# Post-norms of the second block: mean of the early chunks taken off ahead of the last columns

## The chip, the cores and the metric

The kernel runs on one core of one Trainium2 chip, as a single launch. The time is the device time of one execution in microseconds; of several executions the median counts.

## The reference, cut to what matters

Two transformer blocks run one behind the other on 256 tokens of width 1024. The change touches only the second block, whose every sub-layer ends in a layer norm over the residual. All norms of the kernel but the layer norms named below are left alone.

```python
def layer_norm(x):
    xf = x.astype(jnp.float32)
    mu = jnp.mean(xf, axis=-1, keepdims=True)
    var = jnp.mean(jnp.square(xf - mu), axis=-1, keepdims=True)
    return ((xf - mu) * lax.rsqrt(var + EPS)).astype(x.dtype)
def post_norm(x, y):
    return layer_norm(ALPHA * x + y)
def swiglu(h, w_in, w_out):
    gate, up = jnp.split(h @ w_in, 2, axis=-1)
    return (jax.nn.silu(gate) * up) @ w_out
...
    for l in range(DEPTH_2):
        xl = post_norm(xl, 0.5 * g1 * swiglu(modulate(xl, sh1, sc1), ffn1_w_in[l], ffn1_w_out[l]))
        xc = post_norm(xc, 0.5 * cg1 * swiglu(modulate(xc, csh1, csc1), ffn1_w_in[l], ffn1_w_out[l]))
        hl = modulate(xl, sh2, sc2)
        hc = modulate(xc, csh2, csc2)
...
        xl = post_norm(xl, g2 * yl)
        xl = post_norm(xl, 0.5 * g3 * swiglu(modulate(xl, sh3, sc3), ffn2_w_in[l], ffn2_w_out[l]))
        if not last:
            xc = post_norm(xc, cg2 * yc)
            xc = post_norm(xc, 0.5 * cg3 * swiglu(modulate(xc, csh3, csc3), ffn2_w_in[l], ffn2_w_out[l]))
    return xl
```

There are two layers, l=0 with the even mixer and l=1 (`last`) with the odd one; a mixer makes `yc` and `yl` from `hc` and `hl` where the dots are. `modulate(x, shift, scale)` is `x * (1 + scale) + shift`.

## The kernel before

**Layout.** The residual `res` lies feature-major in SBUF: 128 partitions, 8 chunks of 128 features, 512 columns. Columns 0 to 255 are the tokens (s=0), 256 to 511 the context (s=1). `u` (`uhi`, `ulo`) holds the modulated input of the next stage in two parts.

**Projections.** Every projection (`feat`, `toks`) is three matmuls for each pair of 128-blocks: high by high (L224), low by high (L225), high by low (L226). Weights stream through the SP queue (L205) into one of a few buffers `st`; ScalarE casts the high part (L207, `hi`), VectorE makes the low one (L208, `lo`), each into one of three buffers, up to 1024 columns at a time (a unit). A column group g of an output projection gives two chunks of the residual; `gated_add` (L741) adds each chunk from PSUM to `res` on VectorE.

**Where the norms stand.** `post_ln` runs ten times, called here norms 1 to 10 in the order of time. The output loop of `swiglu` makes groups 0 and 1 for all columns, then groups 2 and 3 for each part of 256 columns; behind group 3 of a part it calls `after`, which runs `post_ln` and, chunk by chunk, `modulate` (ScalarE L376, GpSimd L378, VectorE L379). So norms 1 and 2 close the first swiglu (s=0, then s=1), 5 and 6 the second, 7 and 8 the third, 10 the last, where it writes the output instead of modulating. Norms 3 and 4 close the even mixer (s=1, then s=0), whose output comes in four groups of one part (`mix_group`); norm 9 closes the odd mixer. Norms 1 to 8 have projections of the other part or of the next stage on PE beside them. Norms 9 and 10 have none and are made with `solo=True`.

**`post_ln` itself.** GpSimd adds chunks 0 to 5 (L348, L351), VectorE chunks 6 and 7 (in solo these go straight to PE), PE multiplies the sum by a matrix of 1/1024 (`onesm`, L354), which gives the mean spread over all partitions, VectorE subtracts it from pairs of chunks (L356, four of 512 columns). ScalarE squares the eight chunks (L298, in solo L313), VectorE and GpSimd add the squares (L303, L305, in solo L315), PE makes the column sums by matmuls of one column with `ones` (L267; four instructions of PE, sixteen in solo), VectorE adds epsilon (L283, `rc`), GpSimd raises to -1/2 (L286, `pow`, `rr`), PE spreads the result over the partitions (L274, four instructions), VectorE scales each chunk (L365) or, for the output, each pair (L361, then DMA L362).

**What sets the order.** Each engine works through one queue in order. A scheduler writes these queues when the kernel is built: it takes the instructions by priority and by its own model of their durations. Norms have a priority ahead of the code around them (`urgent(NORM)`), `gated_add` another (`EVAC`), the weight split one that draws it ahead (`AHEAD`), norm 9 a further one (`SOLO`). So the written position of a step is not its place in the queue.

## Time and profile before

| | us |
|---|---|
| median of three runs | 2366.41 (2360.74 to 2368.9) |
| the profiled execution | 2360.79 |
| its span | 2359.0 |
| PE busy | 2271.7 (96%) |
| VectorE busy | 1725.5 (73%) |
| ScalarE busy | 1043.4 (44%) |
| GpSimd busy | 233.6 (10%) |

The profile is of one execution. The span runs from its first to its last instruction. PE busy counts matmuls, PEld the weight loads that run beside them; a wait is shown at the instruction that ends it, as [idle before <-what released it]. The clock in a window's row is the granted clock of PE, 1.00 for 2.4 GHz and 0.50 for 1.2 GHz.

### The profile page before, as it was taken

The page shows a single profiled execution, that of the slowest core. Times are in us where ns is not written, and L with a number is a line of the kernel's source. Part 1 is how long each engine was busy: PE and PEld are TensorE (multiplying, and loading weights), DVE is VectorE, ACT ScalarE, POOL GpSimd, SP SyncE. Part 2 cuts the span into 40 slices and gives each one's busy share as a digit, 9 for nine tenths or more (in the row PEclk, how much of TensorE's full clock was granted, in tenths as well). Part 3 has the DMA queues.
Part 4 walks back from the last instruction along what each step waited for, and adds up shares of the span by engine and source line. Part 5 has one row for each costly group of instructions (what it writes and reads, how often), then busy time and mean ns, then how long its engine had stood idle before and what let it go on. Part 6 is the DMA issues. An engine that isn't in the chain of part 4 may idle for free.

```text
span 2359.0 us, 37676 instructions
## 1 busy us (share of the span) xinstructions
PE 2271.7 (96%) x14808; PEld 2032.5 (86%) x14808; DVE 1725.5 (73%) x2757; ACT 1043.4 (44%) x1750; POOL 233.6 (10%) x226
## 2 busy tenths in 40 slices
PE   8999999999999999899899999999999998998998
PEld 7999999998888987667898877998888998887998
DVE  7888887689998654656787776579787477775554
ACT  7765555542222434544442221353232256764442
POOL 1000000200000310211300000220000033101001
PEclk9999999999999999979999999999999999998998
DMA  8546566566666542121455555456555456523653
GB/s 255 164 156 194 170 198 207 186 200 204 193 205 193 166 126 75 40 63 54 129 177 177 156 161 165 156 167 200 174 172 181 130 166 175 139 79 115 186 178 109
DMA packets 336023, 373.96 MB, mean 159 GB/s; under 512 B 12531, under 2 KB 293909, under 8 KB 335846
## 3 DMA queue, kind: packets, MB, share of 16 engines
q1 hardware_dynamic: 335846, 371.56, 51.4%
q8 instruction: 116, 1.90, 0.3%
q14 instruction: 61, 0.50, 0.1%
HBM read 370.37 MB, written 1.14 MB: 157 GB/s over the span
## 4 chain that ended last, share of the span: by engine, by line
PE 62%; DVE 7%; DMA 4%; ACT 3%; issue 2%; POOL 1%; SPq 0%; DVEq 0%; POOLq 0%; ACTq 0%
PE d L224 19%; PE d L225 18%; PE d L226 18%; DMA st<-in_ada_w_dram 3%; DVE ada L403 2%; DVE lo L208 1%; ACT hi L207 1%; PE m L274 1%; PE d L928 1%; PE d L927 1%; PE o L1151 1%; PE o L945 1%; DMA st<-drpb 1%; POOL rr L286 0%; PE m L1197 0%
## 5 line engine op out<-in xcount | busy, mean ns | idle before, releaser
L224 PE MATMUL d<-uhi,hi 128*128 128x256 f32 (+1 forms) x2656 | 865.5, 328 | 5.9 <-ACT uhi L376 2.6
L207 ACT CAST hi<-st 128x1024 fp32r<-128x1024 f32 (+1 forms) x548 | 556.1, 1015 | 707.5 <-PE d L225 548.0
L226 PE MATMUL d<-uhi,lo 128*128 128x256 f32 (+1 forms) x2656 | 865.1, 327 | 2.9 <-DVE lo L208 2.9
L208 DVE TENSOR_TENSOR lo<-st,hi 128x1024 fp32r<-128x1024 f32 (+1 forms) x548 | 656.9, 1200 | 288.2 <-ACT hi L207 285.7
L225 PE MATMUL d<-ulo,hi 128*128 128x256 f32 (+1 forms) x2656 | 865.5, 327 | 1.2 <-DVE ulo L379 1.2
L224 PEld LDWEIGHTS d<-uhi,hi 128*128 128x128 f32 x2656 | 507.1, 192 | 51.1 <-ACT uhi L257 4.2
L226 PEld LDWEIGHTS d<-uhi,lo 128*128 128x128 f32 x2656 | 508.4, 192 | 45.6 <-DVE lo L208 3.7
L225 PEld LDWEIGHTS d<-ulo,hi 128*128 128x128 f32 x2656 | 509.1, 192 | 42.7 <-DVE ulo L379 1.4
L403 DVE SCALAR_TENSOR_TENSOR ada<-st,cs,ada 128x512 f32<-128x512 f32 x504 | 353.4, 747 | 113.8 <-DMA st<-in_ada_w_dram 113.8
L226 PE MATMUL d<-hhi,lo 128*128 128x256 f32 (+1 forms) x1144 | 353.4, 309 | 5.5 <-DVE lo L208 5.5
L224 PE MATMUL d<-hhi,hi 128*128 128x256 f32 (+1 forms) x1144 | 352.7, 308 | 0.0
L225 PE MATMUL d<-hlo,hi 128*128 128x256 f32 (+1 forms) x1144 | 352.3, 308 | 0.0
L226 PEld LDWEIGHTS d<-hhi,lo 128*128 128x128 f32 x1144 | 218.4, 191 | 17.8 <-DVE lo L208 7.3
L225 PEld LDWEIGHTS d<-hlo,hi 128*128 128x128 f32 x1144 | 218.3, 191 | 10.7
L224 PEld LDWEIGHTS d<-hhi,hi 128*128 128x128 f32 x1144 | 218.4, 191 | 10.5
L257 ACT CAST hhi<-hf 128x256 fp32r<-128x256 f32 (+1 forms) x122 | 60.6, 500 | 271.3 <-DVE hf L706 271.3
L348 POOL TENSOR_TENSOR acc<-res 128x256 f32<-128x256 f32 x10 | 11.1, 1113 | 1052.3 <-DVE res L741 1002.2
L224 PE MATMUL d<-hi,uhi 128*128 128x256 f32 x320 | 92.6, 291 | 8.7 <-DVE q L1117 6.4
L378 POOL TENSOR_SCALAR u<-res,sc,mods 128x256 f32<-128x256 f32 x88 | 78.6, 900 | 204.3 <-DVE sc L432 156.2
L225 PE MATMUL d<-lo,uhi 128*128 128x256 f32 x320 | 91.8, 288 | 0.0
L226 PE MATMUL d<-hi,ulo 128*128 128x256 f32 x320 | 91.1, 287 | 0.0
L725 ACT ACTIVATE sg<-d 128x512 f32<-128x512 f32 (+1 forms) x100 | 49.4, 494 | 55.6 <-PE d L226 55.5
(304 smaller groups left out, 2423.2 us busy)
## 6 DMA issues: line engine op xcount, KB each, us to landing
st<-in_ffn_w_in_dram SPq DMA_DIRECT2D x200, 512.0 KB, 4.0
st<-in_ada_w_dram SPq DMA_DIRECT2D x144, 512.0 KB, 3.8
st<-in_ffn_w_out_dram SPq DMA_DIRECT2D x110, 512.0 KB, 3.5
st<-in_na_w_in_dram SPq DMA_DIRECT2D x28, 512.0 KB, 3.9
st<-in_w_in_dram SPq DMA_DIRECT2D x24, 512.0 KB, 5.1
st<-in_w_gate_dram SPq DMA_DIRECT2D x22, 512.0 KB, 3.9
st<-in_w_up_dram SPq DMA_DIRECT2D x22, 512.0 KB, 4.3
st<-in_w_down_dram SPq DMA_DIRECT2D x20, 512.0 KB, 3.9
```

What stands on the lines that cost most here:

```text
L207: nc.scalar.copy(hi[:, :n], st[:, :n])
L208: nc.vector.tensor_sub(lo[:, :n], st[:, :n], hi[:, :n].bitcast(F32))
L224: nc.tensor.matmul(ps, lhi, rhi, start=first, stop=False)
L225: nc.tensor.matmul(ps, lhi, rlo, start=False, stop=False)
L226: nc.tensor.matmul(ps, llo, rhi, start=False, stop=last)
L257: self.nc.scalar.copy(hi, src)
L274: nc.tensor.matmul(ps[:, i * P:(i + 1) * P], col[:, i:i + 1].to_broadcast([P, P]), self.ident, start=True, stop=True)
L378: nc.gpsimd.tensor_scalar(u, z, sc, sh, op0=OP.mult, op1=OP.add)
L403: nc.vector.scalar_tensor_tensor(acc[:, s], st[:, i], c, acc[:, s], op0=OP.mult, op1=OP.add)
L725: nc.scalar.activation(s[:, :t1 - t0], ps[:, :t1 - t0], AF.Silu)
L927: nc.tensor.matmul(ps[:, :w], qn[:, hd, i0:i0 + P], kn[:, hd, ks], start=True, stop=False)
L928: nc.tensor.matmul(ps[:, :w], qr[r, hd // 2, i0:i0 + P], kr[r, ks], start=False, stop=True)
```

## The change

`post_ln` becomes two functions. `ln_begin(t0, n)` is called when the first n chunks of the residual are complete: n=6 behind group 2 of a swiglu's part, n=4 behind group 1 of a mixer. It adds the first half of the n chunks on GpSimd and the second half on VectorE, joins them on VectorE (L353), multiplies by `onesm` (L355, scaled so that it is the mean of these n chunks) and subtracts that from all eight chunks (L358), also from those to which the last groups are yet to be added. Then it squares the n chunks and adds the squares up. `ln_end` is called where `post_ln` was. It squares the remaining 8-n chunks on ScalarE (L368) and gives to PE, one column each, the remaining chunks (for the mean that is left) and all squares (L373). VectorE copies the mean m (L377), squares it (L378) and takes it off the mean square (L379); GpSimd raises to -1/2 (L381). PE spreads m and r (L274), VectorE subtracts m from pairs of chunks (L384) and scales (L393, for the output L389). The flag `solo` no longer reaches the norm; its priority stays at norm 9.

```diff
@@ -339,22 +339,50 @@
         nc.scalar.copy(rs, self.spread(r, T)[:, :T])
         return r, rs
 
-    def post_ln(self, t0, solo=False, chunk=None):
-        nc = self.nc
+    @urgent(NORM)
+    def ln_begin(self, t0, n):
+        nc = self.nc
+        z = [self.res[:, c, t0:t0 + S] for c in range(KD)]
+        h = [self.t(self.tmp, [P, S], "acc", bufs=3) for _ in range(2)]
+        for e, a, (c0, c1) in ((nc.gpsimd, h[0], (0, n // 2)), (nc.vector, h[1], (n // 2, n))):
+            e.tensor_add(a, z[c0], z[c0 + 1])
+            for c in range(c0 + 2, c1):
+                e.tensor_add(a, a, z[c])
+        nc.vector.tensor_add(h[0], h[0], h[1])
+        mb = self.pm()[:, :S]
+        nc.tensor.matmul(mb, self.onesm, h[0], start=True, stop=True)
+        for c in range(0, KD, 2):
+            x = self.res[:, c:c + 2, t0:t0 + S]
+            nc.vector.scalar_tensor_tensor(x, mb[:, None, :].to_broadcast([P, 2, S]), -KD / n, x, op0=OP.mult, op1=OP.add)
+        return n, self.sumsq(z[:n], S)
+
+    def ln_end(self, t0, begun, chunk=None):
+        nc = self.nc
+        n, sq = begun
         z = [self.res[:, c, t0:t0 + S] for c in range(KD)]
         zp = [self.res[:, c:c + 2, t0:t0 + S] for c in range(0, KD, 2)]
-        mb = self.pm()[:, :S]
-        acc = self.t(self.tmp, [P, S], "acc", bufs=3)
-        nc.gpsimd.tensor_add(acc, z[0], z[1])
-        n = KD - 2 if solo else KD
-        for c in range(2, n):
-            (nc.vector if c > 5 else nc.gpsimd).tensor_add(acc, acc, z[c])
-        terms = [acc] + z[n:]
-        for i, x in enumerate(terms):
-            nc.tensor.matmul(mb, self.onesm, x, start=(i == 0), stop=(i == len(terms) - 1))
+        for i, x in enumerate(z[n:]):
+            sq = sq + [self.t(self.tmp, [P, S], "sq" if i < 3 else "u", bufs=3)]
+            nc.scalar.activation(sq[-1], x, AF.Square)
+        ps = self.pm()
+        for o, terms in ((0, z[n:]), (2, sq)):
+            for t in range(2):
+                for i, x in enumerate(terms):
+                    nc.tensor.matmul(ps[:, o + t:o + t + 1], x[:, t * P:(t + 1) * P], self.ones[1024],
+                                     start=(i == 0), stop=(i == len(terms) - 1))
+        c = self.t(self.tmp, [P, 16], "rc")
+        m, m2, var = c[:, 0:2], c[:, 2:4], c[:, 4:6]
+        nc.vector.tensor_copy(m, ps[:, 0:2])
+        nc.vector.tensor_mul(m2, m, m)
+        nc.vector.scalar_tensor_tensor(var, ps[:, 2:4], EPS, m2, op0=OP.add, op1=OP.subtract)
+        r = self.t(self.tmp, [P, 16], "rr")
+        nc.gpsimd.tensor_tensor(r[:, :2], var, self.half[:, :2], op=OP.pow)
+        mb = self.spread(m, S)[:, None, :S].to_broadcast([P, 2, S])
         for x in zp:
-            nc.vector.tensor_sub(x, x, mb[:, None, :].to_broadcast([P, 2, S]))
-        rs = self.rms(z, 1024, S, solo=solo)[:, :S]
+            nc.vector.tensor_sub(x, x, mb)
+        rs = self.spread(r, S)[:, :S]
         if chunk is None:
             ov = self.out.rearrange("(k p) t -> p k t", p=P)
             for i, x in enumerate(zp):
@@ -731,8 +759,10 @@
                 self.rate = orate if g < 2 else 0
                 for n, ps in enumerate(self.feat(wout, KF, g * 256, (P, P), hh, t0, t1)):
                     self.gated_add(ps, 2 * g + n, self.hg[l][:, j3 // 2, 2 * g + n, :], t0, t1)
-                if g == 3:
-                    after(t0 // S)
+                if g == 2:
+                    begun = self.ln_begin(t0, 6)
+                elif g == 3:
+                    after(t0 // S, begun)
 
     @urgent(EVAC)
     def gated_add(self, ps, c, gate, t0, t1):
@@ -747,10 +777,10 @@
             self.gated_add(ps, c, self.mods[l][:, 40 + c, :], s * S, (s + 1) * S)
 
     def then(self, l, j, solo=False):
-        def after(s):
+        def after(s, begun):
             self.need(l, 3 * j + 1)
             with self.tc.high_priority(offset=SOLO if solo else 0):
-                self.post_ln(s * S, solo, lambda c: self.modulate(l, j, s, s * S, (c,)))
+                self.ln_end(s * S, begun, lambda c: self.modulate(l, j, s, s * S, (c,)))
         return after
 
     def block2(self):
@@ -759,7 +789,7 @@
         self.swiglu(0, 2, (1, 0), self.then(1, 0), 0.8, 0.8)
         self.swiglu(1, 1, (0, 1), self.then(1, 1), 0.9, 0.9)
         self.odd(self.then(1, 2, True))
-        self.swiglu(1, 2, (0,), lambda s: self.post_ln(0, solo=True))
+        self.swiglu(1, 2, (0,), lambda s, begun: self.ln_end(0, begun))
         self.su.close()
 
     def even(self, after):
@@ -828,14 +858,21 @@
                 self.gla_norm(0, o, rg, yg)
                 x = yg[0] + ym[0], yg[1] + ym[1]
                 self.need(0, 5)
-                self.mla(mp, 0, ym, qn, qr, kn, kr, vl,
-                         lambda g: self.mix_group(0, a["even_w_out_2"], x, 1, g))
+                begun = []
+
+                def context(g):
+                    self.mix_group(0, a["even_w_out_2"], x, 1, g)
+                    if g == 1:
+                        begun.extend(self.ln_begin(S, 4))
+                self.mla(mp, 0, ym, qn, qr, kn, kr, vl, context)
             self.su = ExitStack()
             self.u = self.hilo(self.pool(self.su, "u2"), KD, 512, "u")
-            after(1)
+            after(1, begun)
             for g in range(4):
                 self.mix_group(0, a["even_w_out_2"], x, 0, g)
-            after(0)
+                if g == 1:
+                    begun = self.ln_begin(0, 4)
+            after(0, begun)
 
     def rope_table(self):
         st = self.t(self.wst, [P, 1024], "st", bufs=NST)
@@ -1264,7 +1301,9 @@
             self.split(u[0][7][:, :S], u[1][7][:, :S], ys[7])
         for g in range(4):
             self.mix_group(1, a["na_w_out_2"], u, 0, g, 6)
-        after(0)
+            if g == 1:
+                begun = self.ln_begin(0, 4)
+        after(0, begun)
 
 
 @with_exitstack
```

Three places show how the queues change. The first is PE's queue where norm 2 is made (`m` is a PSUM tile of the norm, `d` one of a projection; `acc` and `sq` are squares, x2 or x3 counts equal rows; before):

```order
L226 MATMUL d_9356<-hi_9388,ulo_86 128x256
L267 MATMUL m_9212<-ones_97,acc_9189 128x1 x2
L274 MATMUL m_9219<-ident_80,rr_9217 128x128 x2
L224 MATMUL d_9419<-hi_9422,uhi_85 128x256
L225 MATMUL d_9419<-lo_9423,uhi_85 128x256
```

And in the changed kernel:

```order
L224 MATMUL d_9320<-hi_9322,uhi_85 128x256
L373 MATMUL m_9223<-ones_97,res_75 128x1 x3
L373 MATMUL m_9223<-ones_97,acc_9030 128x1
L373 MATMUL m_9223<-ones_97,sq_9219 128x1
L225 MATMUL d_9320<-lo_9323,uhi_85 128x256
L226 MATMUL d_9320<-hi_9322,ulo_86 128x256
L224 MATMUL d_9320<-hi_9322,uhi_85 128x256
L373 MATMUL m_9223<-ones_97,sq_9221 128x1
...
L224 MATMUL d_9319<-hi_9352,uhi_85 128x256
L274 MATMUL m_9240<-ident_80,rc_9234 128x128 x2
L274 MATMUL m_9247<-ident_80,rr_9238 128x128 x2
L225 MATMUL d_9319<-lo_9353,uhi_85 128x256
```

The sums and the spread, which stood together behind the last projection of the part, now stand among its projections: twelve of them lie between the last sum and the spread of m, and the spread of r follows at once. At norms 1, 5, 6, 7 and 8 seven lie there, at norm 4 four.

The second is VectorE's queue at norm 9 (`lo` are weight splits for the last swiglu; before):

```order
L741 SCALAR_TENSOR_TENSOR res_75<-d_21164,mods_103,res_75 128x256
L208 TENSOR_TENSOR lo_21189<-st_21187,hi_21188 128x512
L208 TENSOR_TENSOR lo_21308<-st_21306,hi_21307 128x1024
L741 SCALAR_TENSOR_TENSOR res_75<-d_21185,mods_103,res_75 128x256
L741 SCALAR_TENSOR_TENSOR res_75<-d_21186,mods_103,res_75 128x256
L208 TENSOR_TENSOR lo_21338<-st_21336,hi_21337 128x1024
L356 TENSOR_TENSOR res_75<-res_75,m_21207 128x2x256 x4
```

And in the changed kernel:

```order
L771 SCALAR_TENSOR_TENSOR res_75<-d_21262,mods_103,res_75 128x256
L208 TENSOR_TENSOR lo_21331<-st_21329,hi_21330 128x512
L208 TENSOR_TENSOR lo_21441<-st_21439,hi_21440 128x1024
L208 TENSOR_TENSOR lo_21471<-st_21469,hi_21470 128x1024
L208 TENSOR_TENSOR lo_21507<-st_21505,hi_21506 128x1024
L350 TENSOR_TENSOR acc_21284<-res_75 128x256
L353 TENSOR_TENSOR acc_21283<-acc_21283,acc_21284 128x256
L358 SCALAR_TENSOR_TENSOR res_75<-m_21288,res_75 128x2x256 x4
L771 SCALAR_TENSOR_TENSOR res_75<-d_21305,mods_103,res_75 128x256
L771 SCALAR_TENSOR_TENSOR res_75<-d_21306,mods_103,res_75 128x256
```

The begin part of norm 9 and four gated additions now stand behind four splits, the last of which needs the third buffer to come free; before, two and then one split stood ahead of the last gated additions and of the subtraction.

The third is PE's queue at the end of the program, norm 10 (before):

```order
L226 MATMUL d_23317<-hhi_21302,lo_23470 128x256
L354 MATMUL m_23488<-acc_23489,onesm_89 128x256
L354 MATMUL m_23488<-res_75,onesm_89 128x256 x2
L267 MATMUL m_23522<-ones_97,sq_23504 128x1
L267 MATMUL m_23523<-ones_97,sq_23504 128x1
L267 MATMUL m_23522<-ones_97,sq_23508 128x1
```

And in the changed kernel:

```order
L226 MATMUL d_23479<-hhi_21435,lo_23633 128x256
L373 MATMUL m_23655<-ones_97,res_75 128x1 x4
L373 MATMUL m_23655<-ones_97,acc_23462 128x1
L373 MATMUL m_23655<-ones_97,sq_23651 128x1
L373 MATMUL m_23655<-ones_97,sq_23653 128x1
L373 MATMUL m_23655<-ones_97,acc_23462 128x1
L373 MATMUL m_23655<-ones_97,sq_23651 128x1
L373 MATMUL m_23655<-ones_97,sq_23653 128x1
L274 MATMUL m_23672<-ident_80,rc_23666 128x128 x2
L274 MATMUL m_23679<-ident_80,rr_23670 128x128 x2
```

The mean matmul has left the end: `ln_begin` stands a hundred matmuls ahead. Each row here is two PE instructions in the trace, so the sums behind the last projection are 20.

## Rows read from the trace of the kernel before

**Rows 1.** The page: span, and busy time of each engine

```profile
span 2359.0 us, 37676 instructions
PE 2271.7 (96%) x14808; PEld 2032.5 (86%) x14808; DVE 1725.5 (73%) x2757; ACT 1043.4 (44%) x1750; POOL 233.6 (10%) x226
```

**Rows 2.** Waits of PE: what waited, for what: us in total, times, longest

```profile
PE m L274 <- POOL rr L286: 14.0, 14, 2.1
...
PE m L267 <- DVE acc L305: 8.2, 8, 2.1
...
PE o L1151 <- ACT pth L1144: 1.3, 2, 0.7
```

**Rows 3.** Windows at norms 1 to 8: length, busy time (instructions), clock, DMA

```profile
804.00:830.00 26.00, 24.52 (x203) 24.12 (x203) 20.36 (x34) 13.49 (x23) 13.81 (x13) 1.00 0.50 147
...
1944.00:1972.00 28.00, 22.11 (x159) 21.03 (x158) 22.64 (x42) 14.95 (x28) 12.42 (x13) 0.88 0.66 171
sum 162.00, PE 139.44 PEld 135.19 DVE 120.49 ACT 82.34 POOL 69.85; mean PE 17.43 PEld 16.90 DVE 15.06 ACT 10.29 POOL 8.73
```

**Rows 4.** Timeline at norm 2: start, us, instruction, [idle before <-releaser]

```profile
832.57 0.48 DVE L741 SCALAR_TENSOR_TENSOR res<-d,hg,res 128x256 f32<-128x256 f32 x1
...
845.67 0.58 PE L267 MATMUL m<-ones,acc 128*128 128x1 f32 x4 [1.69 <-DVE acc L305]
847.57 0.90 PE L274 MATMUL m<-ident,rr 128*128 128x128 f32 x4 [1.32 <-POOL rr L286]
849.61 0.58 PE L224 MATMUL d<-hi,uhi 128*128 128x256 f32 x1 [1.15 <-ACT uhi L376]
```

**Rows 5.** Windows of half clock at norms 2, 3, 4, 6, 8

```profile
847.90:854.80 6.90, 5.75 (x28) 5.46 (x27) 5.27 (x14) 3.30 (x6) 5.38 (x8) 0.51 0.24 73
...
sum 27.40, PE 23.07 PEld 22.80 DVE 19.14 ACT 11.23 POOL 17.66; mean PE 4.61 PEld 4.56 DVE 3.83 ACT 2.25 POOL 3.53
```

**Rows 6.** Timeline of PE at norm 1

```profile
809.32 0.60 PE L267 MATMUL m<-ones,acc 128*128 128x1 f32 x4 [1.01 <-DVE acc L305]
...
810.98 0.71 PE L274 MATMUL m<-ident,rr 128*128 128x128 f32 x4 [0.47 <-POOL rr L286]
```

**Rows 7.** One window in the last swiglu, same columns as rows 3

```profile
2300.00:2320.00 20.00, 20.00 (x169) 20.00 (x168) 8.96 (x10) 7.53 (x8) 3.19 (x2) 1.00 0.57 178
```

**Rows 8.** The pow: all of line 286 (min/median/max ns), and timeline at norm 4

```profile
L286 POOL TENSOR_TENSOR rr<-rc,half x20: 695/713/1843, 9.5 to 2350.6; 128x2 f32<-128x2 f32 x18, 128x8 f32<-128x8 f32 x2
...
1176.25 1.23 DVE L208 TENSOR_TENSOR lo<-st,hi 128x1024 fp32r<-128x1024 f32 x1
...
1176.41 1.63 POOL L286 TENSOR_TENSOR rr<-rc,half 128x2 f32<-128x2 f32 x1 [5.88 <-DVE rc L283]
```

**Rows 9.** Timeline of PE behind norm 8

```profile
1959.53 0.55 PE L224 MATMUL d<-hi,uhi 128*128 128x256 f32 x1 [2.89 <-DVE q L1117]
```

**Rows 10.** Timeline at norm 9

```profile
2130.01 1.76 DVE L741 SCALAR_TENSOR_TENSOR res<-d,mods,res 128x256 f32<-128x256 f32 x4 [1.28 <-PE d L226]
...
2136.22 0.70 PE L354 MATMUL m<-acc,onesm 128*128 128x256 f32 x2 [2.96 <-POOL acc L351]
...
2138.31 1.22 DVE L208 TENSOR_TENSOR lo<-st,hi 128x1024 fp32r<-128x1024 f32 x1
...
2142.39 1.84 PE L267 MATMUL m<-ones,sq 128*128 128x1 f32 x8 [3.25 <-DVE sq L315]
...
2148.23 1.08 DVE L365 SCALAR_TENSOR_TENSOR res<-res,m 128x256 f32<-128x256 f32 x3 [2.10 <-PE m L274]
...
2149.34 1.22 PE L224 MATMUL d<-uhi,hi 128*128 128x256 f32 x4 [1.15 <-ACT uhi L376]
```

**Rows 11.** Timeline at norm 10

```profile
2342.52 0.48 DVE L741 SCALAR_TENSOR_TENSOR res<-d,hg,res 128x256 f32<-128x256 f32 x1 [0.23 <-PE d L226]
...
2346.76 1.86 PE L267 MATMUL m<-ones,sq 128*128 128x1 f32 x8 [2.98 <-DVE sq L315]
...
2352.62 2.48 DVE L361 TENSOR_TENSOR res<-res,m 128x512 f32<-128x512 f32 x4 [2.10 <-PE m L274]
```

## Prediction, made before the changed kernel ran

> **What bounds the kernel now.** The page comes first: PE is busy 96% of a span of 2359.0 us [rows 1], and 4% idle is about 87 us for the whole program, so anything that only shortens VectorE, ScalarE or GpSimd work is worth nothing unless PE waits for it. The list of PE's waits says what the norms own of that: 14.0 us for the `pow` on GpSimd ahead of the spread, and 8.2 us for the last addition of the squares ahead of the column sums [rows 2]. Then the windows around the eight norms that have other work beside them, which I call norms 1 to 8 in order of time (first swiglu s=0 and s=1, even mixer s=1 and s=0, third swiglu s=0 and s=1, fourth swiglu s=0 and s=1): over the eight stretches of 162.00 us PE is busy 139.44, so 22.6 us are idle [rows 3]. Norm 2 shows the pattern: the last gated addition begins at 832.57, PE's other matmuls are used up at 844, and PE then waits 1.69 us for the squares, 1.32 us for the `pow` and 1.15 us for the first modulated chunk: 4.16 us [rows 4]. The windows also hold a second loss: after such waits the granted clock falls to half, 0.51 in the window at 847.9. Five stretches of that kind (norms 2, 3, 4, 6, 8) hold 23.07 us of PE busy [rows 5], and work done at 1.2 instead of 2.4 GHz loses half of that, 11.5 us. The two norms with no work beside them, 9 (before the last swiglu) and 10 (output), are read from the timeline below.
>
> **The change, part by part.** The mean of the first n chunks (n=6 behind a swiglu, n=4 behind a mixer) and its subtraction from all eight move ahead of the last column groups, and so do n squares. What stays behind the last gated addition is 8-n squares, the column sums, three narrow VectorE operations, `pow`, two spreads and a second subtraction.
>
> *Removed at norms 1 to 8.* The chain behind the last addition gets shorter by the adds, the mean matmul, the first 2.5 us of subtractions and most squares. At norm 2 the old chain ran from 832.57 to 849.61; even a chain of 10 us would end ahead of 844, where the cover runs out. So the idle time can go, -22.6, and with it the half-clock stretches, -11.5: **-34.1 us**.
>
> *Added on PE.* Column sums of the remaining chunks and of the squares: 20 instructions for n=6 and 36 for n=4, where there were 4. One costs (0.60-0.27)/3 = 0.11 us at full clock, from four in 0.60 us; a spread is four instructions that hold PE for about 0.57 us (0.71 less the overlap with the next) [rows 6]. That is 16x0.11+0.57 = 2.35 us at six norms and 32x0.11+0.57 = 4.1 us at two: **+22.3 us**. It is on the path, since PE is the bound there: a projection matmul takes 0.118 us (169 in 20.00) and in covered stretches nothing else limits [rows 7].
> The Trainium skill, "TensorE: Matmul & The Clock Gate", section Back-to-back issue gap, gives a matmul of 1 to 64 columns about 60 cycles, some 25 ns. By it a sum would cost 0.085 us less, 96 and 64 of them (six norms of 16, two of 32) 13.6 us less, and the forecast would be about 2349. The row speaks against it: four in a row stand 0.11 apart.
>
> *Waits that stay.* From the last sum to the spread of r, norm 1 needed about 1.1 us (809.92 to 810.98, [rows 6]); two more dependent VectorE operations make it about 1.5. In front of that spread now stand 7 projection matmuls, 0.84 us, and the four spread instructions of m, 0.57 us: 0.1 short, taken as 0.25 at norms 1, 5, 6, 7 and 8; norm 2 has 12 matmuls there, none is left; norm 4 has 4, I take 0.5. The `pow` is 0.71 us at its median and was 1.63 at norm 4, where a weight split of 1.23 us ran on VectorE beside it [rows 8]. Now VectorE's next instruction behind the variance waits for the spread of m, so the `pow` is mostly alone and I take 0.71. The Trainium skill, "SBUF — State Buffer", section Who interferes with whom, says that VectorE's second port is GpSimd's and is locked by one of them at a time; the 1.63 us agrees. By it the gain would vanish where a split still lands there, 0.9 us a norm. Norm 8 has 2.89 of its 5.89 us of idle time (28.00-22.11, [rows 3]) on an eviction of the odd mixer's first projections [rows 9], not on the norm; the modulation's eight GpSimd passes now stand ahead of four table additions that wait for DMAs, so I expect most of the rest to go, and leave 1.5. Together **+3.25 us**, between 0 and 10.
>
> *Clock.* The sums are PE instructions that keep it busy but stream one column each. Where they stood in a row in before, they came behind waits, so no row tells which of the two pulled the clock down. Ends: no drop at all (0) or as many as before (11.5); a drop of 3.4 us costs 1.7. I take two to three, mostly at norms 3, 4 and 8: **+4.3 us**.
>
> *VectorE, ScalarE, queues.* Four more subtractions, 2.48 us [rows 11], and three narrow operations a norm on VectorE, which is busy 73% of the span [rows 1]; ahead of them nothing on PE waits at norms 1 to 8, since the splits of weights run a unit or more ahead. Taken as 0; if that cover were gone, 2.5 us a norm. The SP queue has the same DMAs in the same order but for the output. The odd mixer's attention comes out in a somewhat different order; PE waits there 1.3 us for the probabilities [rows 2], and I take no change, within 1.3 either way. Sum for norms 1 to 8: -34.1+22.3+3.25+4.3 = **-4.2 us**.
>
> *Norm 9.* Here the order on VectorE decides. The first half of the mean stands behind a third split of 1024 that waits for its cast, and the cast for a buffer that PE frees. In before that split began at 2138.31, after PE had stood 2.96 us for GpSimd's accumulation until 2136.22 [rows 10]. Without that stop (the mean matmul no longer stands in the middle of a column group) it begins at about 2135.35 and ends at 2136.6. Then two additions (0.8), the mean matmul (0.7), four subtractions (2.48) to 2140.6, four gated additions (1.76) to 2142.35, and 32 of the 36 sums behind them. At 0.21 us (eight in 1.84 at half clock [rows 10]) they end at 2148.6; copy, square and variance to 2149.5; spread of m and subtractions to 2152.7, with `pow` and the spread of r beside them; scale and modulate 1.1 us (2148.23 to 2149.34), PE at 2153.8 instead of 2149.34: **+4.4 us**. At full clock the same steps end at 2150.1, +0.8. I take +4.4, since the sums here ran at half clock before, and PE now idles more ahead of them.
>
> *Norm 10.* The last gated addition ends at 2343.0 in both. Before: mean, subtractions and squares until the sums start at 2346.76, output scaling from 2352.62 [rows 11]. After: square of the last chunk, 20 sums to about 2345.3, variance 2345.9, `pow` to 2346.8, subtractions 2346.65 to 2349.1, scaling from 2349.1: **-3.5 us** (-1.6 with all sums at half clock, -4.4 at best).
>
> **The sum**: -4.2+4.4-3.5 = -3.3 us. Against the profiled execution's own 2360.79 us (span 2359.0 and 1.8 around it) that is 2357.5. The median of the runs shown is 2366.41, 5.6 above that execution, so the forecast for the median is 2366.41-3.3 = **2363 us**. The measurement can tell 0.3%, 7.1 us: this forecast is no change that can be told. With the ends of its unknown terms the forecast reaches from -7.5 (no clock drop, -4.3) to +3 (two drops more and 3 us of waits), 2359 to 2369.
>
> **The rivals.**
> (A) A clean gain. No clock drop (-4.3), norm 9 at full clock (-3.6), norm 8 without a wait (-1.5): -3.3-9.4 = -12.7, **2354**. For it: PE is kept busy through every covered norm. Against it: the sums stand in groups of up to eight, and norm 9's sums come behind idle time. Chance 0.22.
> (A2) The sums cost PE far less than 0.11 us because they overlap with the wide matmuls beside them: 13.6 us less, 2349. Against it are the four at 0.11. The page on TensorE named above is the one that says so. Chance 0.04.
> (B) Slower, by the clock. The narrow sums themselves pull the granted clock to half: one drop at each of the six norms with n=6 and two at the two with n=4, ten drops of 1.7 are 17 us instead of 4.3; norm 10 then gains 1.6 instead of 3.5: -3.3+12.7+1.9 = +11.3, **2378**. It decides from about six drops more than I take, +10.4, at which the time passes 2373.5. For it: at norms 9 and 10 the sums ran at half clock. Against it: at norm 1 four sums and four spreads passed between projections, with 1.5 us of waits, and the window's clock is 1.00 [rows 3, 6]. Chance 0.11.
> (C) The change doesn't start early: at norms 1 to 8 too the begin part stands behind splits, as at norm 9, nothing of the 34.1 comes back, and the added sums hide in half of the 22.6 that stay idle: +22.3-11.3 = +11.0, with norms 9 and 10 +11.9, 2378. The order of the instructions speaks against it; norm 9 is the one place that has it. Chance 0.05.
>
> **How the numbers follow.** Forecast 0.56, A 0.24, A2 0.04, B 0.11, C 0.05. The range leaves out A2, B and C, which are 0.20, and ends a little beyond A's 2354 and halfway from the forecast's own upper end to B: **2353 to 2374**. Faster by over 0.3% (under 2359.3): most of A, A2 and the low edge of the forecast, 0.29. Slower by over 0.3% (over 2373.5): B and C, 0.16, less the part of B with fewer drops, 0.14. Same: 0.57.
>
> **What would show it.** In the windows of norms 1 to 8 idle time near 3 us in place of 22.6, some 22 us more PE busy in narrow instructions, the clock near 1.00 with two or three dips; no wait of PE for a last addition of squares. At norm 9 the first mean addition at 2136 to 2137 behind a split, and PE's next stage 4 us later. At norm 10 the scaling about 3.5 us earlier after the last projection. A sum at 0.03 us would make it wrong towards faster, half clock at each norm towards slower.

## The result: slower, by more than was left in the range

The changed kernel took 2376.74 us at the median of ten runs (2373.4 to 2385.12), the kernel before 2367.37 us at the median of ten (2357.12 to 2369.99). The ratio is 1.0057 with a 95% interval of 1.0042 to 1.0072. The forecast was 2363 us and no change that can be told; the time lies 2.7 us above the upper end of its range.

The page of the changed kernel, the lines that answer to [rows 1], from an execution of 2385.03 us:

```profile
span 2382.9 us, 38103 instructions
PE 2301.0 (97%) x15024; PEld 2058.5 (86%) x15024; DVE 1745.0 (73%) x2815; ACT 1042.4 (44%) x1750; POOL 191.0 (8%) x184
```

216 PE instructions were added (15024 less 14808), and PE is busy 97% instead of 96%: idle time has been turned into work, as the change means to, and the span is longer. The spans differ by 23.9 us, the medians by 9.4: the profiled execution of before (2360.79) lies 6.6 us under its median, that of the changed kernel 8.3 over its own. How much of the 23.9 belongs to the change is read by letting the two traces run beside each other on the same projections. Both kernels make the same 4274 matmuls of high by high part (L224) in nearly the same order; the time between two of them, in one kernel less the other, is what a stretch gained or lost. Worked out so from the traces (microseconds against before, + is slower; the names of the experiments are those of the next section):

```
stretch (projections)        after  vg_first  before_vg  n9_solo  n9_few  few_vg  direct   join
up to norm 1 (0-1620)         +9.3    +1.2      +2.3      +4.6     +3.8    +2.9    +3.1    +2.1
norm 1 (1620-1716)            +2.9    +2.2      +1.5      +2.2     +2.2    +2.6    +2.6    +1.6
norm 2 (1716-1790)            +4.7    -4.7      +1.9      -4.7     -4.7    -3.2    -4.7    -4.0
norms 3, 4 (1945-2110)        +0.1     0.0       0.0       0.0     +0.4    -2.7    +0.3    -6.3
norm 5 (2640-2716)            +2.2    +2.2       0.0      +2.2     +3.2    +2.6    +3.5    +1.6
norm 6 (2716-2790)            -1.8    -1.8       0.0      -1.8     -1.8    -1.4    -1.8    -2.4
norm 7 (3310-3380)            +2.2    +2.2       0.0      +3.0     +2.2    +2.6    +2.6    +1.6
norm 8 (3380-3690)            -3.3    +0.6      +1.3      -2.7     -1.7    +0.1    -1.4    -1.9
norm 9 (3740-3757)            +4.7    +4.7      -1.3      +2.0     +0.1    +0.1    +0.7    +0.6
last projection to the end    -3.6    -3.5       0.0      -3.0     -4.0    -3.9    -3.3    -3.5
```

The first row holds the same instructions in the same order in every kernel, apart from norm 1's mean matmul at its end, some 0.6 us (two matmuls and 1.0 us in `direct`): the rest of the 1.2 to 9.3 us are differences between executions. The execution of before that stands ahead of the prediction was the quickest of all in it, the one of after the slowest. The norms' own stretches of after add up to +8 us (without the first row), close to the 9.4 us of the medians. The stretches that the table leaves out add 7.6 us in after, 4.1 of them in the even mixer, where `only_n10`, with nothing changed there, has 3.5.

The longest waits of PE in the changed kernel (us in total, times, longest us), to be laid beside [rows 2]:

```profile
PE d L226 <- DVE lo L208: 12.2, 7, 5.1
PE m L355 <- DVE acc L353: 7.4, 5, 3.1
PE d L224 <- DVE vg L825: 6.2, 1, 6.2
...
PE m L274 <- POOL rr L286: 4.0, 5, 1.1
PE m L373 <- DVE res L771: 3.4, 2, 3.1
```

The waits for the last addition of squares and, but for 0.3 us at norm 4, for the `pow` of these norms are gone (what L286 makes here belongs to other norms). In their place stand two others: the mean matmul of the begin part (L355) waits for the joined chunk sums (L353), and once PE waits 6.2 us for `vg`, which is no part of a norm. That is the stretch of norm 2 (timeline; start, duration, and what ended the idle time):

```profile
854.07 0.41 DVE L393 SCALAR_TENSOR_TENSOR res<-res,m 128x256 f32<-128x256 f32 x1
...
854.66 1.64 POOL L406 TENSOR_SCALAR u<-res,sc,mods 128x256 f32<-128x256 f32 x1 [6.18 <-DVE res L393]
...
863.84 0.43 DVE L407 TENSOR_TENSOR ulo<-u,uhi 128x256 fp32r<-128x256 f32 x1 [0.38 <-POOL u L406]
864.18 0.74 DVE L393 SCALAR_TENSOR_TENSOR res<-res,m 128x256 f32<-128x256 f32 x2
...
864.84 0.42 DVE L825 COPY vg<-d 128x256 f32<-128x256 f32 x1
...
865.40 0.55 PE L224 MATMUL d<-hi,uhi 128*128 128x256 f32 x1 [6.16 <-DVE vg L825]
```

`vg` holds the even mixer's first projections (of the other part), which VectorE copies out of PSUM. PE's next group waits for the PSUM tile that the copy sets free. On VectorE that copy stands behind the scaling (L393, eight instructions) and most of the modulation (L407, six of eight) of norm 2, from 854.07 to 864.84. These steps are paced by GpSimd's `u` (L406), one chunk after the other, and three weight splits of 1.2 us stand among them. In before the norm was still adding up its squares when the copies came due, and four of them went ahead of its scaling (VectorE, before):

```profile
841.41 0.41 DVE L795 COPY vg<-d 128x256 f32<-128x256 f32 x1
...
845.11 0.41 DVE L305 TENSOR_TENSOR acc<-acc,acc 128x256 f32<-128x256 f32 x1
...
848.50 1.08 DVE L365 SCALAR_TENSOR_TENSOR res<-res,m 128x256 f32<-128x256 f32 x3 [1.78 <-PE m L274]
```

The clock, in the windows of half clock at norms 1 to 8 (columns as [rows 3]; [rows 5] are those of before):

```profile
809.70:813.10 3.40, 3.40 (x18) 3.40 (x18) 1.76 (x2) 1.04 (x1) 0.68 (x1) 0.50 0.16 55
847.30:850.70 3.40, 3.40 (x18) 3.40 (x17) 0.49 (x4) 1.04 (x1) 0.71 (x1) 0.50 0.47 147
864.30:871.20 6.90, 5.80 (x27) 5.83 (x28) 2.83 (x8) 1.35 (x3) 1.33 (x2) 0.51 0.20 68
1154.50:1157.90 3.40, 3.40 (x17) 3.40 (x17) 1.21 (x5) 1.04 (x1) 0.71 (x1) 0.50 0.02 5
1181.80:1185.20 3.40, 3.40 (x18) 3.40 (x18) 0.44 (x2) 0.29 (x1) 1.59 (x3) 0.50 0.44 145
sum 20.50, PE 19.40 PEld 19.43 DVE 6.72 ACT 4.77 POOL 5.02; mean PE 3.88 PEld 3.89 DVE 1.34 ACT 0.95 POOL 1.00
```

PE busy at half clock is 19.40 us instead of 23.07, so work worth 9.7 us at full clock is lost instead of 11.5. The third window follows the wait for `vg`; the other four follow no long wait but the column sums of norms 1 to 4. Not all of the loss reaches the time: norm 1's stretch is 0.7 us longer than in the kernels without that drop (+2.9 against +2.2), since the wait of the mean matmul behind it shrank from 1.5 to 1.0 us.

Norm 9, on VectorE and PE:

```profile
2151.74 1.76 DVE L771 SCALAR_TENSOR_TENSOR res<-d,mods,res 128x256 f32<-128x256 f32 x4 [1.28 <-PE d L226]
...
2157.60 1.23 DVE L208 TENSOR_TENSOR lo<-st,hi 128x1024 fp32r<-128x1024 f32 x1 [0.21 <-ACT hi L207]
2158.74 0.42 DVE L350 TENSOR_TENSOR acc<-res 128x256 f32<-128x256 f32 x1
...
2159.74 0.70 PE L355 MATMUL m<-acc,onesm 128*128 128x256 f32 x2 [3.14 <-DVE acc L353]
2160.48 2.48 DVE L358 SCALAR_TENSOR_TENSOR res<-m,res 128x512 f32<-128x512 f32 x4 [0.79 <-PE m L355]
...
2163.50 3.55 PE L373 MATMUL m<-ones,res 128*128 128x1 f32 x16 [3.06 <-DVE res L771]
...
2172.82 2.48 DVE L384 TENSOR_TENSOR res<-res,m 128x512 f32<-128x512 f32 x4 [0.92 <-PE m L274]
...
2176.40 0.48 DVE L407 TENSOR_TENSOR ulo<-u,uhi 128x256 fp32r<-128x256 f32 x1
```

The begin part's addition comes right behind the last split, at 2158.74, and everything else of the norm behind that. Norm 10:

```profile
2369.98 0.48 DVE L771 SCALAR_TENSOR_TENSOR res<-d,hg,res 128x256 f32<-128x256 f32 x1 [0.23 <-PE d L226]
...
2372.73 0.16 DVE L377 COPY rc<-m 128x2 f32<-128x2 f32 x1 [2.26 <-PE m L373]
...
2376.55 2.47 DVE L389 TENSOR_TENSOR res<-res,m 128x512 f32<-128x512 f32 x4
```

From the last gated addition to the output's scaling there are 6.57 us, where [rows 11] had 10.10 (2342.52 to 2352.62): 3.5 us less.

### The profile page after: what moved, and what is told of

Same layout as the page of the kernel before. It is cut to its first block, busy times and chain, and to the rows that moved or that the text cites. A ratio compares the mean times of both kernels' runs of the same rounds, so it can differ in the third digit from the quotient of the medians.

```text
span 2382.9 us, 38103 instructions
## 1 busy us (share of the span) xinstructions
PE 2301.0 (97%) x15024; PEld 2058.5 (86%) x15024; DVE 1745.0 (73%) x2815; ACT 1042.4 (44%) x1750; POOL 191.0 (8%) x184
## 4 chain that ended last, share of the span: by engine, by line
PE 46%; DVE 18%; DMA 9%; issue 4%; ACT 2%; POOL 1%; DVEq 0%; POOLq 0%; ACTq 0%
PE d L224 13%; PE d L225 13%; PE d L226 13%; DMA st<-in_ada_w_dram 9%; DVE ada L431 6%; DVE lo L208 4%; DVE adt L437 1%; PE m L373 1%; POOL u L406 1%; DVE adr L438 1%; DVE hf L734 1%; PE m L274 1%; DVE hlo L258 1%; PE d L965 1%; PE d L964 1%
## 5 line engine op out<-in xcount | busy, mean ns | idle before, releaser
L224 PE MATMUL d<-uhi,hi 128*128 128x256 f32 (+1 forms) x2656 | 864.5, 327 | 5.7 <-ACT uhi L404 2.4
L208 DVE TENSOR_TENSOR lo<-st,hi 128x1024 fp32r<-128x1024 f32 (+1 forms) x548 | 650.1, 1187 | 268.5 <-ACT hi L207 264.6
L224 PEld LDWEIGHTS d<-uhi,hi 128*128 128x128 f32 x2656 | 506.3, 191 | 50.3 <-ACT uhi L257 4.1
L224 PE MATMUL d<-hhi,hi 128*128 128x256 f32 (+1 forms) x1144 | 355.0, 310 | 0.0
L226 PEld LDWEIGHTS d<-hhi,lo 128*128 128x128 f32 x1144 | 219.3, 192 | 23.9 <-DVE lo L208 13.2
L224 PEld LDWEIGHTS d<-hhi,hi 128*128 128x128 f32 x1144 | 219.1, 192 | 10.6
L406 POOL TENSOR_SCALAR u<-res,sc,mods 128x256 f32<-128x256 f32 x88 | 88.7, 1017 | 246.3 <-DVE sc L460 156.2
L224 PE MATMUL d<-hi,uhi 128*128 128x256 f32 x320 | 92.5, 291 | 10.7 <-DVE vg L825 6.2
L224 PEld LDWEIGHTS d<-hi,uhi 128*128 128x128 f32 x320 | 62.6, 196 | 12.8 <-ACT uhi L404 6.3
```

Of the source, the lines that this page charges most:

```text
L208: nc.vector.tensor_sub(lo[:, :n], st[:, :n], hi[:, :n].bitcast(F32))
L224: nc.tensor.matmul(ps, lhi, rhi, start=first, stop=False)
L226: nc.tensor.matmul(ps, llo, rhi, start=False, stop=last)
L406: nc.gpsimd.tensor_scalar(u, z, sc, sh, op0=OP.mult, op1=OP.add)
```

## The experiments

All ratios are against the kernel before, run beside it on the same chip. A kernel of the list is named by its label; line numbers in a row are those of that kernel's own program.

**vg_first: is it the order at norm 2?** Only the eight evictions are moved ahead.

```diff
-        nc.vector.tensor_copy(vg[:, t, i * 256:(i + 1) * 256], ps[:, :256])
+        with self.tc.high_priority(offset=EVAC):
+            nc.vector.tensor_copy(vg[:, t, i * 256:(i + 1) * 256], ps[:, :256])
```

> The changed kernel with one thing moved: the eight evictions of the even mixer's first projections (VectorE, vg<-d) get the priority of the gated additions. Theory (order at norm 2): in the changed kernel PE stood 6.16 us at 865 for such an eviction, which stood on VectorE behind the whole scaling and modulation of norm 2, and lost another 3.4 us by 6.8 us of half clock behind it. Then this kernel is 6 to 9.6 us faster than the changed one, at +0 to +3.5 us against before, and the wait on vg is under 1 us. Rival (the narrow sums and their clock make the loss, the wait only moves to the modulated chunks): within 2 us of the changed kernel, +7 to +11 against before, with a wait for uhi or ulo in place of the one for vg.

Measured: 1.0016 (0.9998 to 1.0033), a median of 2368.9 us. That is 0.4% under the changed kernel's ratio, some 9.7 us, and the two intervals do not overlap. In the trace norm 2 goes from +4.7 to -4.7 us, and its window has 0.3 us of idle time left and full clock:

```profile
832.00:863.00 31.00, 30.73 (x246) 29.21 (x245) 23.29 (x45) 14.54 (x20) 8.15 (x9) 1.00 0.50 137
```

The two traces differ by 9.3 us at norm 2, but not all of it is the late evictions': about 1.6 us are the drop of the clock at 847.30, ahead of the wait. `covered` and `n9_old` (below) have the same order at norm 2 and the same wait, shown here for both, but not that drop:

```profile
PE d L225 <- DVE vg L857: 6.1, 1, 6.1
```

Their norm 2 stands at +2.1 and +2.9. So the late evictions cost 6.7 to 7.8 us, the clock behind the wait included, and without them norm 2 comes out where the forecast's terms had put it: 2.35 of sums and spread, -4.16 of idle time and -2.9 of half clock (half of 5.75, [rows 5]) are -4.7.

**before_vg: the control.** The same edit in the kernel before.

> The kernel before with the priority of the gated additions for the same eight evictions, nothing else. Theory (the wait is made by the changed norm, which has VectorE's queue full of scaling where the evictions come due): in before no wait on vg exists at norm 2, so 0 +- 1 us at norm 2 and in the sum. Rival (the evictions were late in before as well, hidden in the 4.16 us of waits): norm 2 gets 2 to 4 us faster here too, and the gain of the earlier experiment is no evidence on the change.

Measured: 1.0019 (1.0 to 1.0037). Norm 2 got 1.9 us slower, more than the 1 us that the theory allows and not faster, as the rival has it; its sums waited longer, since the evictions now stood ahead of the additions of squares:

```profile
850.50 0.98 PE L267 MATMUL m<-ones,acc 128*128 128x1 f32 x4 [2.99 <-DVE acc L305]
```

In [rows 4] that wait was 1.69 us. The rival is out: the late eviction is a thing of the changed norm.

**covered and n9_old: which norms lose.** In `covered` norms 9 and 10 are made as before, in `n9_old` norm 9 alone; the old function stands beside the new ones.

```diff
-                begun = self.ln_begin(0, 4)
+                begun = self.ln_begin(0, 4) if 9 in NEW else None
...
-                self.ln_end(s * S, begun, lambda c: self.modulate(l, j, s, s * S, (c,)))
+                put = lambda c: self.modulate(l, j, s, s * S, (c,))
+                if begun is None:
+                    self.post_ln(s * S, solo, put)
+                else:
+                    self.ln_end(s * S, begun, put)
```

> The changed norm at norms 1 to 8 alone; norms 9 and 10 as before. Theory: the windows of the two traces give +9 at norms 1 and 2, 0 at 3 and 4, +1 at 5 and 6, -2 at 7 and 8, together +8 us against before. The prediction's own sum was -4.2. A result near -4 would say that the profiled execution was disturbed there; near +8 that the loss is systematic.

> The changed kernel with norm 9 as it was before (mean, squares and sums behind the last gated addition), all other norms as changed. Theory: norm 9 lost 4.4 us (its next projection started 27.0 us later than in before, and the step in front of it 22.4), so this kernel is about 4.4 us faster than the changed one, +5 against before. Rival (the loss at norm 9 is the attention in front of it, which came out in another order): no gain, +9 against before.

Measured: `covered` 1.0043 (1.0024 to 1.0062), about +10 us at the median (2374.04 against 2364.17): the loss at norms 1 to 8 is systematic. `n9_old` 1.0030 (1.0008 to 1.0051): 0.27% under the changed kernel, 6.4 us, with wide intervals; in its trace norm 9 stands at 0.0 against before, so the attention in front of it is not what made the loss.

**only_n10: the output norm alone.** The kernel before with the new functions at the last norm.

> The kernel before with the changed norm at norm 10 alone. Theory: the output scaling starts 3.5 us earlier behind the last projection, -3.5 us against before. Rival (the begin part in the covered stretch costs PE or its clock as much): -1 to +1.

Measured: 0.9992 (0.997 to 1.0014), too close to one to tell. In the trace the end came 3.9 us sooner behind the last projection, and 0.5 us of that was paid ahead of it, for the mean matmul. The stretches of norms 1 to 9 are within 0.3 us of before; the stretch ahead of norm 1 (+5.5) and the even mixer's (+3.5) are not, with the same instructions.

**n9_solo: late begin or many sums?** On top of `vg_first`, norm 9's begin part gets the priority of its end part.

```diff
             if g == 1:
-                begun = self.ln_begin(0, 4)
+                with self.tc.high_priority(offset=SOLO):
+                    begun = self.ln_begin(0, 4)
```

> The changed kernel with the evictions first and with norm 9's begin part at the priority of its end part, so that its additions and subtractions stand ahead of the last two splits on VectorE. Theory (late begin): the four gated additions behind it end about 2.5 to 3 us earlier, and norm 9's stretch (the 17 projection groups around it) loses 2 us against before instead of 4.65. Rival (36 narrow sums at half clock and the longer chain behind them make the loss): the stretch still loses 4 to 4.65 us.

Measured: norm 9 loses 2.0 us instead of 4.7, as the theory had it (1.0014, 0.9998 to 1.0029, for the whole). PE no longer waits for the mean matmul, and the sums begin sooner behind the first gated additions (8.8 us behind them instead of 11.8, 2135.63 to 2144.42 here and 2151.74 to 2163.50 in the changed kernel):

```profile
2135.63 1.76 DVE L771 SCALAR_TENSOR_TENSOR res<-d,mods,res 128x256 f32<-128x256 f32 x4 [1.28 <-PE d L226]
...
2140.21 0.59 PE L355 MATMUL m<-acc,onesm 128*128 128x256 f32 x2
...
2144.42 0.35 PE L373 MATMUL m<-ones,res 128*128 128x1 f32 x2 [3.62 <-DVE res L771]
...
2146.33 2.72 PE L373 MATMUL m<-ones,res 128*128 128x1 f32 x12 [0.53 <-DVE res L771]
```

**n9_few: 8 sums in place of 36 at norm 9.** On top of `n9_solo`:

```diff
+        zs = z[n:]
+        if solo:
+            a = self.t(self.tmp, [P, S], "acc", bufs=3)
+            nc.vector.tensor_add(a, zs[0], zs[1])
+            for x, q in zip(zs[2:], sq[1:]):
+                nc.vector.tensor_add(sq[0], sq[0], q)
+                nc.vector.tensor_add(a, a, x)
+            for q in sq[3:]:
+                nc.vector.tensor_add(sq[0], sq[0], q)
+            sq, zs = sq[:1], [a]
         ps = self.pm()
-        for o, terms in ((0, z[n:]), (2, sq)):
+        for o, terms in ((0, zs), (2, sq)):
...
```

> As the kernel before this one in the list (evictions first, norm 9's begin part urgent), and at norm 9 the four last squares and the four last chunks are added up on VectorE, so that PE makes 8 sums instead of 36. Theory (each sum costs 0.21 us at half clock on norm 9's path): 28 sums less are 5.9 us, the additions give 2.5 back, so 3 us faster at norm 9 than with the begin part urgent alone, about -1 against before. Rival (sums cost far less than that, or hide): no gain or a loss of 1 to 2 us from the additions.

Measured: norm 9 at +0.1 us, 1.9 us better than with 36 sums, not the 3 expected (1.0002, 0.9982 to 1.0021). PE waits for the additions until just before the eight sums:

```profile
2148.31 1.83 PE L383 MATMUL m<-ones,acc 128*128 128x1 f32 x8 [8.72 <-DVE acc L375]
```

**few_vg: 8 sums at norms 1 to 8.** On top of `vg_first`, norm 9 as before; the last squares are added on VectorE and the last chunks on GpSimd at norms 1 to 8.

```diff
+        zs = z[n:]
+        if chunk is not None:
+            for x in sq[1:]:
+                nc.vector.tensor_add(sq[0], sq[0], x)
+            a = self.t(self.tmp, [P, S], "sq", bufs=3)
+            nc.gpsimd.tensor_add(a, zs[0], zs[1])
+            for x in zs[2:]:
+                nc.gpsimd.tensor_add(a, a, x)
+            sq, zs = sq[:1], [a]
...
```

> The changed norms 1 to 8 and 10 with the evictions first, norm 9 as before, and at norms 1 to 8 the last squares (VectorE) and the last chunks (GpSimd) added up, so that PE makes 8 sums a norm instead of 20 and 36. Theory (0.105 us a sum, PE is the bound there): 6x12 and 2x28 sums less are 13.4 us at norms 1 to 8 and about -13 us against before in all (ratio 0.994 to 0.996). Rival (a sum costs about 0.025 us beside wide matmuls): 3 us less. Second rival (the additions delay the column sums on VectorE and GpSimd): waits for the sums' operands come in their place.

Measured: 0.9991 (0.9973 to 1.0009). The second rival was right: at norms 1, 5 and 7 the stretches got 0.4 us slower than in `vg_first`, because six norms now wait 1.2 us for GpSimd's addition (1.57 us long at its median) and most of them 0.4 us more for the `pow`.

```profile
PE m L409 <- POOL sq L401: 7.1, 6, 1.2
...
PE m L382 <- DVE acc L380: 4.2, 3, 1.4
```

**direct: the wait of the mean matmul.** On top of `n9_few`, the sixth chunk goes to PE by itself.

```diff
-        for e, a, (c0, c1) in ((nc.gpsimd, h[0], (0, n // 2)), (nc.vector, h[1], (n // 2, n))):
+        for e, a, (c0, c1) in ((nc.gpsimd, h[0], (0, n // 2)), (nc.vector, h[1], (n // 2, min(n, 5)))):
...
-        nc.tensor.matmul(mb, self.onesm, h[0], start=True, stop=True)
+        nc.tensor.matmul(mb, self.onesm, h[0], start=True, stop=n < 6)
+        if n == 6:
+            nc.tensor.matmul(mb, self.onesm, z[5], start=False, stop=True)
```

> As the kernel with 8 sums at norm 9 (evictions first, norm 9's begin part urgent), and behind the swiglus the sixth chunk goes straight to PE as a second mean matmul instead of through two more additions on VectorE. Theory (the mean matmul of norms 2, 6 and 8 makes PE wait 1.5 us, because behind the last gated addition of its group a weight split of 1.2 us and three additions stand on VectorE): these waits shrink to under 0.5 us, the second matmul costs 0.3 us at six norms, net 2 to 3 us faster. Rival (VectorE is late there for the gated addition itself, behind the scaling of the norm before): the waits stay at 1 to 1.5 us, net 1 to 2 us slower.

Measured: 0.9997 (0.9984 to 1.001), which can't be told from `n9_few` or from before; in the traces norms 1, 5 and 7 lose 0.3 to 0.5 us more than in `n9_few`. The rival was right. The waits stay at 1.1 to 1.5 us, and the rows of VectorE at norm 2 say why:

```profile
817.83 0.43 DVE L419 TENSOR_TENSOR ulo<-u,uhi 128x256 fp32r<-128x256 f32 x1 [0.38 <-POOL u L418]
818.17 0.48 DVE L783 SCALAR_TENSOR_TENSOR res<-d,hg,res 128x256 f32<-128x256 f32 x1
818.57 1.22 DVE L208 TENSOR_TENSOR lo<-st,hi 128x1024 fp32r<-128x1024 f32 x1
819.70 0.48 DVE L783 SCALAR_TENSOR_TENSOR res<-d,hg,res 128x256 f32<-128x256 f32 x1
820.10 1.22 DVE L208 TENSOR_TENSOR lo<-st,hi 128x1024 fp32r<-128x1024 f32 x1
821.23 0.42 DVE L350 TENSOR_TENSOR acc<-res 128x256 f32<-128x256 f32 x1
821.68 0.42 DVE L353 TENSOR_TENSOR acc<-acc,acc 128x256 f32<-128x256 f32 x1
```

The gated addition itself follows norm 1's last modulation step without a gap, so it was late, and two splits stand between it and the first addition of the mean.

**join: 12 and 20 sums.** On top of `n9_few`: at norms 1 to 8 only the squares are added up, on VectorE.

```diff
+        elif chunk is not None:
+            for q in sq[1:]:
+                nc.vector.tensor_add(sq[0], sq[0], q)
+            sq = sq[:1]
```

> As the kernel with 8 sums at norm 9, and at norms 1 to 8 the last squares alone are added up on VectorE (the chunks still go to PE one by one), so that PE makes 12 sums instead of 20 and 20 instead of 36. Theory (0.105 us a sum): 6x8 and 2x16 sums less are 8.4 us, and without the addition on GpSimd, which made a wait of 1.18 us at six norms, most of it comes through: 6 to 8 us faster. Rival (any operand that is later makes a wait of the same size): 0 to 2 us.

Measured: 0.9949 (0.9930 to 0.9969), a median of 2356.38 us against 2366.93: faster than the changed kernel and than before. Against `n9_few` the stretches of the table give 8.5 us, where the theory said 6 to 8; the largest part came at norms 3 and 4, 6.7 us. 32 sums less are 3.4 us of that, and the rest is the clock: their windows at `n9_few` and at `join`:

```profile
1130.00:1152.00 22.00, 21.74 (x178) 21.26 (x177) 15.60 (x30) 8.37 (x12) 4.78 (x6) 1.00 0.39 120
1152.00:1186.00 34.00, 33.65 (x259) 33.45 (x259) 25.02 (x49) 18.99 (x31) 8.37 (x10) 0.90 0.43 131
```

```profile
1125.00:1147.00 22.00, 22.00 (x186) 21.59 (x185) 15.82 (x29) 9.17 (x13) 4.61 (x6) 1.00 0.32 99
1148.00:1178.00 30.00, 29.21 (x243) 28.80 (x243) 26.56 (x50) 17.41 (x28) 4.49 (x8) 1.00 0.48 149
```

The clock of the second pair is 1.00 throughout; in the first it is 0.90 in the window of 34 us, a tenth of it or 3.4 us of work lost. Norms 1 and 7 gained 0.6 us each (8 sums less, less a wait of 0.4 us for the `pow`), norm 5 1.6, since it had a drop of the clock in `n9_few`; norm 2 lost 0.7.

**best: `join` and `direct` together.**

> Both of the two edits before this one in the list, together with the evictions first and norm 9's begin part urgent with 8 sums. Theory: the gains add up to 8 to 10 us, with norm 10's 3 us about -9 to -12 us against before (0.995 to 0.996). If one of the two edits only moves its wait, half of that.

Measured: 0.9951 (0.9931 to 0.9972), a median of 2358.5 us: no better than `join`, as `direct` alone gave nothing.

## Why the prediction was wrong, point by point

**What bounds the kernel, and what goes.** Right about the old waits: they went, and the begin part started early at norms 1 to 8, so rival C did not come. But new waits took their place. PE's idle time in the seven stretches of norms 1 to 8 is 26.1 us in before, 16.9 in the changed kernel and 14.2 in `vg_first`.

**The price of a sum, 0.11 us.** Right. Norm 5's stretch has 20 PE instructions more (258 instead of 238) and as much idle time as before (1.55 and 1.47 us), and takes 2.17 us longer, 0.11 us for each. Rival A2, and with it the Trainium skill's 25 ns ("TensorE: Matmul & The Clock Gate", Back-to-back issue gap, which gives it for an isolated matmul) as the price of these sums, is out. At norm 1 of the changed kernel ten sums in a row take 1.04 us (806.57 to 807.61):

```profile
806.57 0.73 PE L373 MATMUL m<-ones,res 128*128 128x1 f32 x6
807.16 0.36 PE L373 MATMUL m<-ones,acc 128*128 128x1 f32 x2
807.38 0.36 PE L373 MATMUL m<-ones,sq 128*128 128x1 f32 x2
807.61 0.36 PE L225 MATMUL d<-hlo,hi 128*128 128x256 f32 x1
```

**"VectorE, ScalarE, queues ... Taken as 0."** This is the step that failed. It counted what the norm adds on VectorE and saw that the weight splits run early enough. It did not ask what else the moved norm now comes ahead of on that queue. A norm whose scaling starts earlier puts fourteen instructions, six of them fed by GpSimd chunk by chunk, ahead of evictions for which PE waits: 6.2 us of wait at norm 2 and half clock behind it, 6.7 to 7.8 us in all by `vg_first` beside the three kernels with the late evictions, with the control `before_vg`. Without this loss the time lies inside the stated range (`vg_first`, 2368.9). The prediction read such evictions once, at norm 8 ([rows 9], `q` of the odd mixer), and took them as someone else's wait.

**Waits that stay, 3.25 us.** Too small by the mean matmul's wait, which has no term in the sum at all: 1.0 us at norm 2, 1.5 us each at norms 6 and 8, in the stretches of norms 1, 5 and 7. By its terms norms 1, 5 and 7 were to lose 1.1 us each; they lost 2.2 or more. `direct` took away one of the three additions behind the last gated addition, and the wait stayed; that the queue ahead of them makes it is read from VectorE's rows. The `pow` was right: where before had 1632 ns at norms 3, 4 and 6, with a weight split beside each, all ten now take 707 to 721 ns (min/median/max):

```profile
L381 POOL TENSOR_TENSOR rr<-rc,half x10: 707/707/721, 809.7 to 2373.4; 128x2 f32<-128x2 f32 x10
```

By the Trainium skill ("SBUF — State Buffer", Who interferes with whom) it had to be alone on the shared port for that, and the trace agrees: VectorE runs nothing beside nine of them, and beside norm 4's only a subtraction with one of its inputs in PSUM.

**Clock, 4.3 us.** Too small for the changed kernel, where 9.7 us were lost, half of the 19.40 us of PE busy in the five windows; 2.9 of them stand behind the wait for `vg`. With that wait gone, `vg_first` has three drops, at norms 3, 4 and 8 (from 1134.5, 1161.8 and 1970.8), 10.2 us of PE busy at half clock or 5.1 us lost, close to the term. Norms 3 and 4 were named rightly: all seven kernels with 36 sums at them have 6.8 us of half clock there, two drops of 3.4 or one of 6.8, and the two with 20 sums (`join`, `best`) have none. `join` differs from `n9_few`, and `best` from `direct`, only by squares added up on VectorE in place of 16 sums a norm, so at these two norms it is the number of sums. At norms 1, 5 and 7 it isn't settled: with 20 sums a drop of 3.4 us comes 7 times in the 21 passes of these seven kernels, in no fixed place, and with 12 sums not in the 6 passes of the other two. Rival B was therefore half right in its mechanism, but not at every norm, and that its time of 2378 came near to the measured one is luck.

**Norm 9, +4.4 us.** Right: +4.7. By `n9_solo` 2.7 us of it are the late begin part; by `n9_few` another 1.9 went when additions took the place of 28 sums at half clock. So rival A, which had norm 9 at full clock and no drop at norms 1 to 8, did not come either.

**Norm 10, -3.5 us.** Right: -3.5, less 0.6 us ahead of it for the mean matmul that moved there.

**The sum.** For norms 1 to 8 the forecast was -4.2 us; the stretches of the changed kernel give +6.9 and those of `vg_first` +0.7. The two differ by the 9.3 us at norm 2 and 0.7 of clock at norm 1, less 3.9 by which norm 8 came out better in the first of these executions. Of the 4.9 us that still lie between `vg_first` and the forecast, 3.2 stand at norms 1, 5 and 7, where the three mean matmuls wait 1.5 us each; this is read from the traces and not shown by an edit, since `direct` did not take the wait away. Norm 8 is 3.0 us worse there than the forecast's terms, which give -2.4 with one drop of the clock, and norms 3, 4 and 6 are about 2 better. Norm 8 came out between -3.3 and -1.1 in the six other kernels with 20 sums there, so its part may be the execution; no run separates the two. With the -4.2 replaced by +6.9 the working's own sum is +7.8, 2374.2: the measured median is 2.5 us above it.

**The range** took the waits' upper end as 3 us more than the forecast. With the end of 10 that the same paragraph had named for them, and 2.5 us for norm 2's cover, the forecast's own upper end is 2363+3.4+6.75+2.5 = 2375.7 instead of 2369, and halfway from there to rival B is 2377. Rival A stands there with two chances, 0.22 and 0.24; only with the second do the five add up to one.

## What to carry to other kernels

Work that is taken off a chain early also takes its place in the queues early. Before an in-order engine is called free at that point, list what was ahead of the moved step and now comes behind it, and who waits for that: here copies out of PSUM. Where PE is the bound, a sum by a one-column matmul cost nearly as much here as a projection's matmul of 256 columns (0.10 to 0.11 us against 0.118). Adding the operands on an engine with slack first paid where the sums did not come to wait for that addition: VectorE for the squares paid, GpSimd for the chunks, at 1.57 us each, did not.

## What the runs showed that was not expected

The same instructions in the same order ahead of norm 1, some 780 us, took 1.2 to 9.3 us longer in every other profile than in the one of before (0.6 of it the mean matmul in most), eight of the twelve with more half clock, and all but one with longer waits for weight splits. Of the 24 us between the two profiles the greater part was of this kind. The stretches that the change touches, each taken between the same two projections, repeat far better: norm 2 at -4.67 to -4.69 in three kernels with the same code there, norm 6 at -1.78 to -1.79 in six. Norm 8's stretch, 180 us long, does not: with nothing changed there it is +1.3 in `before_vg` and -0.1 in `only_n10`.

At norms 3 and 4, 36 narrow sums that alternate with projections brought half clock in the changed kernel (from 1154.5 and 1181.8) with no wait of PE of over 0.4 us near it. The eight sums of `few_vg` had it too, there behind a wait of 2.88 us.
